# A prefix sum of row blocks: the last two groups by rows, with their columns taken by TensorE

## The chip, the cores and the metric

One core of a Trainium2 chip. The metric is the time of one execution on the device, in microseconds, as the median of several runs; lower is better. A profile gives the span from the first to the last instruction; measured times are about 1.7 us longer than it (677.9 against 676.2 for the run before).

## The reference

```python
def reference(x):                        # x: 4 x 4224 x 4224, float32
    ps = np.cumsum(np.cumsum(x, axis=1), axis=2)
    diag = np.diagonal(ps, axis1=1, axis2=2)
    return np.cumsum(diag, axis=1).astype(np.float32)
```

Only the diagonal of the 2-d prefix sum is wanted, and its running sum. A step of the diagonal from i-1 to i adds the new row up to the diagonal and the new column above it. So the kernel has to read every element once (285 MB) and form sums of rows left of the diagonal and sums of columns above it.

## The kernel before

The matrix of a batch is cut into 11 groups of 384 rows. A group is loaded as a strip, 128 partitions with 3 rows each. For each group

- ScalarE sums each row up to the end of the diagonal block (`act_sum`, which writes its input back in place);
- VectorE masks the diagonal block, sums what is above the diagonal, and adds the three rows into `u`, the running column sums;
- TensorE multiplies the group's 384 columns of `u` with a selecting weight, which puts their sum over the partitions into row k of `d` (`columns`).

The last batch ends otherwise: group 9 is loaded by rows, group 10 in pieces (`part_a`, `part_b`) whose sums on VectorE stand behind `d` in its queue: those of `part_a`'s first piece before the two scans of `d`, the rest after them. The names at the end: `r3` is what remains of the groups' row sums and goes into `d` too, `pu` and `c12` are sums and scans of `d`, `arows` and `bsum` the row sums of `part_a` and `part_b`, and `fin_a`, `fin_b`, `fin_e` the products that weigh them into the last results `yl` and `ye`.

```python
def act_sum(acc, src):
    nc.scalar.activation(out=src, in_=src, func=ACT.Copy, accum_out=acc)

def pair_sum(acc, src):            # VectorE adds two halves and accumulates
    w = src.shape[-1] // 2
    pair = dumpool.tile([P, 768], FP32, name="pair")
    nc.vector.scalar_tensor_tensor(out=pair[:, :w], in0=src[:, :w], scalar=1.0,
        in1=src[:, w:], op0=ALU.mult, op1=ALU.add, accum_out=acc)
# ... cut ...
for g in range(NG if whole else LG - 1):        # NG = 11, LG = 10
    # ... strip loaded whole ...
    for q in range(F):                          # F = 3
        act_sum(rsum[:, k, q : q + 1], strip[:, q, :hi])
    block = strip[:, :, lo:hi]
    nc.vector.tensor_mul(out=block, in0=block, in1=um3)
    row_sums(rabove[:, k, :], block)
    # ... group 0 cut: u = sum of the rows ...
    for q in range(F):
        add_to(u[:, lo:], strip[:, q, lo:])
    columns(g, u_of(g))
if not whole:
    columns(LG, head[:, 0, :])
    g = LG - 1
    # ... cut ...
    wa = 2304
    for q in range(F):
        load(out=strip[:, q, :], in_=rows_of(b, g)[:, q, :])
    for q in range(F):
        act_sum(rsum[:, k, q : q + 1], strip[:, q, :wa])
        pair_sum(more[:, q : q + 1], strip[:, q, wa:hi])
        block = strip[:, q, lo:hi]
        masked(block, block, um3[:, q, :], rabove[:, k, q : q + 1])
        add_to(u[:, lo:], strip[:, q, lo:])
    for j in (g, LG):
        columns(j, u_of(j))
    add_to(rsum[:, k, :], more)
# ... r3 into d, loads of group 10, pu and c12 from d, carry ...
        sum_a(1, *acuts[0], acuts[0][0] + 1536)   # ScalarE's share of part_a
# ... two scans, then ...
sum_a(3, *acuts[1], acuts[1][0] + 768)
# ... arows, fin_a, fin_b, then part_b and the end ...
```

## Time and profile before

| | before |
|---|---|
| time, median | 677.86 us (4 runs, 677.56 to 678.51) |
| span of the profiled run | 676.2 us |
| last piece of the input lands | 665.8 us |
| `d` ready, VectorE starts `pu` | 663.8 us |
| TensorE starts `fin_a` | 669.4 us |

The transfers set the pace up to 665.8; 10.4 us of the span lie after them. The lines that show it, and the chain of waits at the end, stand in the prediction below. One view that it tells in words is the table of stretches of 1 us. Its columns are the stretch, its length, the busy time with instruction counts of TensorE, its weight loads, VectorE, ScalarE and GpSimd, the granted TensorE clock, the transfer engines' share, and GB/s:

```profile
662.00:663.00 1.00, 1.00 (x4) 0.41 (x3) 0.00 (x0) 1.00 (x3) 0.00 (x0) 0.50 0.99 388
...
664.00:665.00 1.00, 0.04 (x2) 0.07 (x3) 1.00 (x4) 0.52 (x3) 0.00 (x0) 1.00 0.15 60
```

The second-last figure falls from 0.99 to 0.15: the stream is over. VectorE (the third pair) is idle at 662, waiting for `d`, just when it should work off what has landed.

### The profile page before, as it was taken

What the parts mean: (1) busy time and instruction counts of PE and PEld (TensorE: products, weight loads), DVE (VectorE), ACT (ScalarE), POOL (GpSimd) and SP (SyncE); (2) the same over time, 40 slices, a digit from 0 to 9 for tenths busy, and PEclk for the clock granted to TensorE, in tenths of its full rate; (3) what the DMA queues carried; (4) which work ended last, traced back from release to release, by engine and by line L of the source; (5) the groups of instructions that cost most, each with busy time, mean ns of one, the idle gap of its engine ahead of it and who ended that gap; (6) DMA issues with size and microseconds to landing.
All of it is one profiled execution on the core that took longest, in us unless ns stands there. A gap on an engine that the chain in (4) does not pass through costs nothing.

```text
span 676.2 us, 1095 instructions
## 1 busy us (share of the span) xinstructions
PE 73.6 (11%) x138; PEld 12.8 (2%) x138; DVE 449.0 (66%) x277; ACT 276.3 (41%) x275; POOL 35.0 (5%) x81
## 2 busy tenths in 40 slices
PE   0001100000010000000100000001101000001015
PEld 0000000000000000000000000000000000000002
DVE  3679766544379887655347988765334998875475
ACT  0023344456622233445761223346674122345673
POOL 5000000000000000000000000000000000001200
PEclk9999999999999999999999999999999555555556
DMA  9999999999999999999999999999999999999992
GB/s 371 432 435 435 432 435 435 435 441 435 438 435 432 435 432 432 432 432 432 432 432 432 432 432 432 432 435 432 432 432 432 435 432 432 432 432 430 416 418 101
DMA packets 7868, 285.62 MB, mean 422 GB/s; under 512 B 872, under 2 KB 1300, under 8 KB 1844
## 3 DMA queue, kind: packets, MB, share of 16 engines
q0 software_dynamic: 7392, 284.89, 97.7%
q1 hardware_dynamic: 468, 0.66, 0.3%
q14 instruction: 7, 0.06, 0.0%
q8 instruction: 1, 0.02, 0.0%
HBM read 285.47 MB, written 0.07 MB: 422 GB/s over the span
## 4 chain that ended last, share of the span: by engine, by line
DMA 73%; ACT 10%; DVE 9%; issue 6%; PE 2%; ACTq 0%; DVEq 0%; POOLq 0%
DMA strip<-in_x_dram 73%; ACT strip L211 10%; DVE u L231 4%; DVE u L300 1%; DVE strip L297 1%; DVE above L214 1%; PE d L205 1%; DVE pair L220 1%; DVE c L379 0%; PE fin_b L205 0%; DVE strip L234 0%; PE fin_a L205 0%; DVE pu L214 0%; DVE c L234 0%; ACTq L211 0%
## 5 line engine op out<-in xcount | busy, mean ns | idle before, releaser
L211 ACT ACTIVATE strip<-strip 128x768 f32<-128x768 f32 (+11 forms) x137 | 270.5, 1975 | 389.0 <-DMA strip<-in_x_dram 374.7
L231 DVE TENSOR_TENSOR u<-u,strip 128x3840 f32<-128x3840 f32 (+10 forms) x121 | 299.1, 2472 | 2.9
L297 DVE TENSOR_TENSOR strip<-strip,um 128x1152 f32<-128x1152 f32 x42 | 57.0, 1357 | 203.4 <-ACT strip L211 203.4
L205 PE MATMUL d<-u,sel 128*33 128x384 f32 (+1 forms) x88 | 65.0, 844 | 593.9 <-DVE u L231 593.9
L214 DVE TENSOR_REDUCE above<-strip 128x3 f32<-128x1152 f32 x42 | 56.8, 1353 | 1.5
L292 POOL DMA_DIRECT2D strip<-in_x_dram x39 | 20.7, 530 | 574.6 <-DVE u L231 535.8
L211 ACT ACTIVATION_READ_ACCUMULATOR strip<-strip 128x1 f32 x137 | 25.5, 186 | 0.0
L205 PEld LDWEIGHTS d<-u,sel 128*33 128x33 f32 (+1 forms) x88 | 7.6, 134 | 648.7 <-DVE u L231 647.7
L300 DVE TENSOR_TENSOR u<-strip 128x4224 f32<-128x4224 f32 x4 | 18.2, 4549 | 0.0
L220 DVE SCALAR_TENSOR_TENSOR pair<-strip 128x384 f32<-128x384 f32 (+5 forms) x12 | 6.9, 577 | 0.2
L214 DVE TENSOR_REDUCE pu<-d 33x1 f32<-33x384 f32 (+1 forms) x2 | 1.1, 548 | 6.1 <-PE d L205 6.1
L198 DVE TENSOR_SCALAR steps<-steps 128x128 int32<-128x128 int32 x1 | 0.2, 227 | 7.0 <-POOL steps L197 7.0
L352 POOL DMA_DIRECT2D strip<-in_x_dram x5 | 2.7, 552 | 4.7 <-DMA strip<-in_x_dram 4.7
L205 PE MATMUL d<-ones_all,r 128*33 128x128 f32 (+1 forms) x12 | 2.6, 377 | 0.0
L316 POOL DMA_DIRECT2D strip<-in_x_dram x3 | 1.6, 528 | 14.2 <-issue 14.2
L205 PE MATMUL fin_b<-weights,bsum 128*1 128x128 f32 (+2 forms) x12 | 2.1, 362 | 0.0
L341 POOL DMA_DIRECT2D strip<-in_x_dram x2 | 1.4, 709 | 13.2 <-issue 13.2
L379 DVE TENSOR_TENSOR_SCAN c<-ones_all,carry,c 33x384 f32<-33x384 f32 (+1 forms) x2 | 2.0, 1008 | 0.1
L379 DVE TENSOR_TENSOR_SCAN c<-ones_all,carry,d 33x384 f32<-33x384 f32 (+1 forms) x2 | 2.0, 1003 | 0.1
L205 PEld LDWEIGHTS d<-ones_all,r 128*33 128x33 f32 (+1 forms) x12 | 1.8, 154 | 2.2 <-issue 1.9
L205 PE MATMUL fin_a<-weights,arows 128*1 128x256 f32 (+1 forms) x4 | 1.4, 514 | 3.9 <-DVE arows L214 3.9
L86 POOL DMA_DIRECT2D strip<-in_x_dram x3 | 1.7, 594 | 0.8 <-POOLq L467 0.8
(67 smaller groups left out, 28.5 us busy)
## 6 DMA issues: line engine op xcount, KB each, us to landing
strip<-in_x_dram POOLq DMA_DIRECT2D x42, 6336.0 KB, 27.9
strip<-in_x_dram POOLq DMA_DIRECT2D x3, 2112.0 KB, 22.3
strip<-in_x_dram POOLq DMA_DIRECT2D x1, 2304.0 KB, 18.7
strip<-in_x_dram POOLq DMA_DIRECT2D x1, 1536.0 KB, 21.8
strip<-in_x_dram POOLq DMA_DIRECT2D x3, 480.0 KB, 23.0
head<-in_x_dram SPq DMA_DIRECT2D x1, 576.0 KB, 3.9
strip<-in_x_dram POOLq DMA_DIRECT2D x1, 352.0 KB, 23.7
strip<-in_x_dram POOLq DMA_DIRECT2D x1, 128.0 KB, 19.0
```

The costliest lines, as they stand in the source:

```text
L86: load(out=t, in_=rows_of(0, i))
L205: nc.tensor.matmul(o, lhsT=lhsT, rhs=rhs, start=start, stop=False, skip_group_check=True)
L211: nc.scalar.activation(out=src, in_=src, func=ACT.Copy, accum_out=acc)
L214: nc.vector.reduce_sum(out=acc, in_=src, axis=AX.X)
L220: nc.vector.scalar_tensor_tensor(out=pair[:, :w], in0=src[:, :w], scalar=1.0, in1=src[:, w:], op0=ALU.mult, op1=ALU.add, accum_out=acc,)
L231: nc.vector.tensor_add(out=o, in0=o, in1=i)
L292: load(out=strip, in_=rows_of(b, g))
L297: nc.vector.tensor_mul(out=block, in0=block, in1=um3)
L300: nc.vector.tensor_add(out=u, in0=strip[:, 0, :], in1=strip[:, 1, :])
L316: load(out=strip[:, q, :], in_=rows_of(b, g)[:, q, :])
L352: load(out=part_b[:, sb, c0:c1], in_=x[b, r0 : r0 + R, :NH].rearrange("r (k c) -> r k c", k=4)[:, :, c0:c1],)
L379: nc.vector.tensor_tensor_scan(out=c12[:, i, :], data0=ones_row[:rows], data1=src, initial=carry[:, i : i + 1], op0=ALU.mult, op1=ALU.add,)
```

## The change

The intent is to have VectorE ready when the last rows land. Groups 8 and 9 are loaded by rows; ScalarE sums only 2176 columns of each, so that VectorE's part doesn't wait for it; TensorE takes the columns from the strip itself, which saves the adds into `u`; and VectorE, now freer, gets more of the last sums. Group 0's row sums go from ScalarE to VectorE as well. The core of the diff (the `pair` tile grows from 768 to 896 columns, too):

```diff
-        for g in range(NG if whole else LG - 1):
+        for g in range(NG if whole else LG - 2):
 ...
+            if g == 0:
+                row_sums(rsum[:, k, :], block)
+            else:
+                for q in range(F):
+                    act_sum(rsum[:, k, q : q + 1], strip[:, q, :hi])
 ...
+            for j in range(LG - 2, NG):
+                columns(j, u_of(j))
             columns(LG, head[:, 0, :])
-            g = LG - 1
-            wa = 2304
 ...
-                add_to(u[:, lo:], strip[:, q, lo:])
-            for j in (g, LG):
-                columns(j, u_of(j))
+            wa = 2176
+            for i, g in enumerate((LG - 2, LG - 1)):
+                k, lo, hi = row_of(g), g * GW, (g + 1) * GW
+                strip = strip_tile()
+                for q in range(F):
+                    load(out=strip[:, q, :], in_=rows_of(b, g)[:, q, :])
+                for q in range(F):
+                    act_sum(rsum[:, k, q : q + 1], strip[:, q, :wa])
+                    pair_sum(more[:, i, q : q + 1], strip[:, q, wa:hi])
+                    block = strip[:, q, lo:hi]
+                    masked(block, block, um3[:, q, :], rabove[:, k, q : q + 1])
+                    for j in range(g + 1, NG):
+                        columns(j, strip[:, q, j * GW : (j + 1) * GW])
+                    columns(g, block)
+                add_to(rsum[:, k, :], more[:, i, :])
 ...
-            sum_a(1, *acuts[0], acuts[0][0] + 1536)
+            sum_a(1, *acuts[0], acuts[0][0] + 1216)
-        sum_a(3, *acuts[1], acuts[1][0] + 768)
+        sum_a(3, *acuts[1], acuts[1][0] + 640)
-        for k, ca in ((0, 480), (1, 480), (2, 416)):
+        for k, ca in ((0, 416), (1, 416), (2, 416)):
```

More of the change, by code (lines that the diff above doesn't have):

```diff
@@ L218, in pair_sum @@
         w = src.shape[-1] // 2
-        pair = dumpool.tile([P, 768], FP32, name="pair")
+        pair = dumpool.tile([P, 896], FP32, name="pair")
         nc.vector.scalar_tensor_tensor(
@@ L293 @@
             k, lo, hi = row_of(g), g * GW, (g + 1) * GW
-            for q in range(F):
-                act_sum(rsum[:, k, q : q + 1], strip[:, q, :hi])
             block = strip[:, :, lo:hi]
+            if g == 0:
[3 more added lines that the diff above has]
+                    act_sum(rsum[:, k, q : q + 1], strip[:, q, :hi])
             nc.vector.tensor_mul(out=block, in0=block, in1=um3)
@@ L307 @@
         if not whole:
+            for j in range(LG - 2, NG):
+                columns(j, u_of(j))
             columns(LG, head[:, 0, :])
-            g = LG - 1
-            k, lo, hi = row_of(g), g * GW, LG * GW
-            strip = strip_tile()
-            more = last.tile([P, F], FP32, name="more")
-            wa = 2304
-            for q in range(F):
-                load(out=strip[:, q, :], in_=rows_of(b, g)[:, q, :])
-            for q in range(F):
-                act_sum(rsum[:, k, q : q + 1], strip[:, q, :wa])
-                pair_sum(more[:, q : q + 1], strip[:, q, wa:hi])
-                block = strip[:, q, lo:hi]
-                masked(block, block, um3[:, q, :], rabove[:, k, q : q + 1])
-                add_to(u[:, lo:], strip[:, q, lo:])
-            for j in (g, LG):
-                columns(j, u_of(j))
-            add_to(rsum[:, k, :], more)
+            more = last.tile([P, 2, F], FP32, name="more")
+            wa = 2176
[13 more added lines that the diff above has]
+                add_to(rsum[:, k, :], more[:, i, :])
         if b < LB - 1:
```

## The prediction

> **What bounds the kernel now.** I read the page's slices first, to see whether any engine or the transfers are full:
>
> ```profile
> DVE  3679766544379887655347988765334998875475
> DMA  9999999999999999999999999999999999999992
> q0 software_dynamic: 7392, 284.89, 97.7%
> ```
>
> The transfer engines are at nine tenths or more in 39 of 40 slices, and queue 0 takes 97.7% of the span. No compute engine is full over the run (VectorE 66%, ScalarE 41%, TensorE 11%). So up to the last bytes the kernel can't become faster by any saving of instructions: the change moves the same bytes. What can be saved is the time between the last landing and the end. Next I looked for when the last bytes come: in stretches of one microsecond the transfer share falls from 0.99 (662 to 663 us) to 0.34 and 0.15; the issues by line show the last piece (128 KB) issued at 646.81 and landing 19.0 us later, at 665.8. The span is 676.2. So 10.4 us at the end run without transfers. The chain of waits, in order of time, says what fills the end:
>
> ```profile
> 608.94 27.49 DMA strip<-in_x_dram
> 636.54 5.00 ACT strip L211 x3
> 642.59 3.26 ACT strip L211 x3
> 645.88 1.37 DVE strip L297
> 647.27 1.35 DVE above L214
> ...
> 660.14 3.64 PE d L205 x10
> 663.80 0.55 DVE pu L214
> ...
> 669.44 1.44 PE fin_a L205 x4
> 670.88 2.76 PE fin_b L205 x16
> 673.66 0.29 DVE yl L418
> ...
> 674.04 0.18 DVE ye L451
> ```
>
> From 636.5 the chain isn't DMA any more. Group 8 lands whole at 636.5; ScalarE sums its three rows of 3456 columns in place until 645.9; only then may VectorE mask the block, and it is 8 us late from there on. The timeline of that stretch shows it:
>
> ```profile
> 645.88 1.36 DVE L297 TENSOR_TENSOR strip<-strip,um 128x1152 f32<-128x1152 f32 x1 [7.97 <-ACT strip L211]
> 648.54 4.13 DVE L231 TENSOR_TENSOR u<-u,strip 128x1152 f32<-128x1152 f32 x3
> 651.63 2.12 ACT L211 ACTIVATE strip<-strip 128x2304 f32<-128x2304 f32 x1 [1.57 <-DMA strip<-in_x_dram]
> 652.59 0.95 DVE L220 SCALAR_TENSOR_TENSOR pair<-strip 128x768 f32<-128x768 f32 x1
> 660.14 2.73 PE L205 MATMUL d<-u,sel 128*11 128x384 f32 x4 [4.68 <-DVE u L231]
> ```
>
> VectorE starts group 9 at 652.6 though its last row landed at 651.6, ends it at 660.1, TensorE makes d until 663.8, and everything that VectorE still owes (sums of part_a and part_b) stands behind d in its queue.
>
> **What the Trainium skill says.** "DMA: Bandwidth & Descriptors", Where 436 GB/s comes from, puts the ceiling of this path at 435.2 GB/s; the page's slices show 432 to 435 nearly throughout, so it agrees and the stream has no reserve. "VectorE: DVE Perf Modes", The perf-mode tier table, has fp32 tensor_tensor at 1x, one element a cycle: here 384 columns take 0.56 us and 768 take 0.95, a slope of 1.0 ns a column, which agrees; I size the new pair sums by it. "TensorE: Matmul & The Clock Gate", What's actually happening: the array runs at 1.2 GHz until it has been busy about 3.4 us, then at 2.4, and falls back after such a window of idleness. The trace agrees at the end: TensorE is busy from 660.14, the granted clock goes from 0.50 to 1.00 at about 663.2, and back to 0.50 at about 666.6; at 1.00 a 128x128 half took 270 ns, at 0.50 it took 418. (The 0.97 of the first 558 us I don't believe: the 384-column halves took 848 ns there and 831 later at 0.50.) "FP8 and Floating Point Precision" tells of four passes for a true fp32 product; no separate run shows passes here, but one column call is two MATMULs, issued 0.63 us apart at clock 0.50, 1.27 us a call.
>
> **The change, part by part.**
>
> Loading: group 8 in three row pieces of 2112 KB. Group 9's already went so, at 641.6, 646.7 and 651.6, 5.0 us apart, 15.1 for the strip where whole strips take 15.0. Group 8's rows should land at about 626.5, 631.5, 636.5. Cost 0 to 0.1 us. The GpSimd queue waits on earlier landings for its last issues; by the order of waits of both kernels, the last two pieces wait for the first and second row of group 9 in both, so the last landing stays 665.8.
>
> Group 0's sums: 3 activations (3 x 0.5 us) become one reduction of 1152 columns, 1.35 us, on VectorE in each batch. In the last batch VectorE is behind there: its group 2 ends at 564.4 and then idles 1.75 us for ScalarE. 1.35 fits into 1.75, and the strips in flight reach to 546 while the delayed load would be issued at 537. Worth 0.
>
> ScalarE in groups 8 and 9: it is done with group 7 at 629.9. Six sums of 2176 columns at about 2.0 us plus the readout, against 3 x 3.07 and 3 x 2.12 before: rows 8 end at 632, 634.1, 638.7, rows 9 at 643.7, 648.7, 653.8 (landing plus 2.2).
>
> VectorE: removed are, for group 8, the mask (1.37), the reduction (1.35) and three adds (4.13), for group 9 three adds of 0.96; added are three pair sums of width 640 (0.86 start to start), three masks (0.60), and pair sums of 832 in place of 768 (1.06 against 0.99). Group 8 costs 3 x 1.46 = 4.4 in place of 6.85, and, as the pair sums and masks read columns that ScalarE does not touch, it starts when VectorE is free of group 7, at 637.9, not at 645.9: done 642.4. Group 9 then goes with its landings, 644.1, 648.2, 653.3. The row sums are whole at 653.9, r3 at 654.1; before, 660.2.
>
> TensorE: from 637.95 it has 5 calls (u 7 to 10 and head), then 9 for group 8, 6 for group 9, where it had 5 in all from 652.7. 20 calls at 1.27 would be 25.4 us, 663.4. But it is busy without a gap from 637.95, so I expect the clock to rise at about 641.5; the 2.7 calls done by then leave 11.3 of the first 14, at 0.65 us (half of 1.27, an estimate) 7.3 us: 648.8. Group 9's six then follow their rows, the last block at about 653.9; r3 0.6 to 1.1. d is ready at about 655.0 against 663.8: 8.8 us earlier.
>
> The end: pu and c12 1.2, 656.2. The next in VectorE's queue, the pair sums of part_a, wait for a landing at 657.25; two of width 544 at 0.75: 658.75. Carry and two scans 2.2: 661.0. Second piece (660.95), two of width 448 at 0.65: 662.3; arows 662.55. TensorE starts fin_a at 662.75 instead of 669.44. From fin_a's start to the finish of fin_b took 673.66 - 669.44 = 4.22 us, TensorE without a gap; part_b's pieces land at 662.6 to 665.5 and the pair sums of width 272 take 0.46, so the inputs come in time: 666.97. VectorE is done with the last piece (665.8 + 0.4 + what stands before it) at 666.3, just earlier. From there to the end before: 676.2 - 673.66 = 2.54. New span 669.5, a gain of 6.7; measured times are 1.7 above the span (677.87 against 676.2): 671.2. Of the 8.8 us won at d, 1.0 goes to the wait for part_a at 657.25, the rest to wider sums and landings. The cuts of ScalarE's share cost VectorE 2 x 0.17 + 2 x 0.07 + 2 x 0.03, about 0.5 us, and it has waits to put them in.
>
> **The rivals.** First, TensorE stays cold in the run of 20 calls: d at 663.4 plus 1.1, 664.6, 0.8 later than before, and the wider pair sums add 0.5 behind it: 679. For: it has never been busy longer than 4 us in this trace, and at 652.73 to 655.46, busy 2.7 us, it stayed at 0.50. Against: both bursts over 3 us ended at 1.00. A part of it (clock rises late, or falls between group 9's rows) costs 1 to 3 us, of which the wait for part_a hides the first: 671.5 to 674. Second, the landings hide the gain: the end can't be before 665.8 + 0.4 (last pair sum) + 0.3 (fin_e) + 2.3 (ye to the end), 668.8, time 670.5. That's only 0.7 below my figure, so it is a floor and not another outcome. Third, the smaller loads or the later strip release slow the stream: 0.1 to 0.5 us per group seen against; the page's slice with group 9's rows has 416 GB/s against 432, which would be 0.6: 671.8.
>
> **Range and chances.** The floor is near below, the rivals stretch upward: 671.2, eight in ten within 670.3 to 673.6. Faster by 2% would be 664.3, below the floor: 0.01. Slower by 2% is 691.4; even the cold case is far from it: 0.01.
>
> **What would show it.** Right: the last landing still near 665.8; VectorE's first group 8 pair sum at about 638 with no wait for ScalarE; granted clock at 1.00 from about 641 to 655; pu near 655 followed by a wait for a transfer; fin_a near 662.8. Wrong: column halves still 0.63 us apart after 645, pu after 660, or transfers below 430 GB/s between 605 and 660.

## The result, and the profile after

The changed kernel took 671.43 us (4 runs, 670.94 to 671.47) against 677.86; the ratio is 0.9902, with a 95% interval from 0.9885 to 0.9919. A ratio here and below is the mean time of one kernel's fast runs over that of the kernel before in the same rounds, so it is not quite the ratio of the medians quoted. Predicted were 671.2, within 670.3 to 673.6. The span is 669.7 (predicted 669.5).

The chain of waits of the changed kernel, in order of time (start, length, what):

```profile
626.90 6.94 ACT strip L211 x7
...
639.12 21.96 DMA strip<-in_x_dram
...
662.74 0.17 DVE arows L214
...
662.96 1.44 PE fin_a L205 x4
664.40 2.76 PE fin_b L205 x16
...
667.18 0.29 DVE yl L424
...
667.56 0.18 DVE ye L457
```

The long run of VectorE and TensorE pieces from 645.9 to `fin_a` at 669.4 is gone. Between 639 and 661 the chain is a transfer again: that of `part_a`'s second piece. After it come ScalarE's sums, `arows`, and the same 4.2 us of products (`fin_a`, `fin_b`) as before, 6.5 us sooner: 662.96 against 669.44.

The timeline of the changed kernel, whose brackets give how long the engine idled before and for whom:

```profile
637.78 0.82 DVE L220 SCALAR_TENSOR_TENSOR pair<-strip 128x640 f32<-128x640 f32 x1
637.92 5.30 PE L205 MATMUL d<-u,sel 128*11 128x384 f32 x8 [13.32 <-DVE u L231]
643.70 9.19 PE L205 MATMUL d<-strip,sel 128*11 128x384 f32 x28
...
651.73 1.02 DVE L220 SCALAR_TENSOR_TENSOR pair<-strip 128x832 f32<-128x832 f32 x1 [3.43 <-DMA strip<-in_x_dram]
653.41 0.82 PE L205 MATMUL d<-strip,sel 128*11 128x384 f32 x2 [0.52 <-DVE strip L234]
655.18 0.55 DVE L214 TENSOR_REDUCE pu<-d 11x1 f32<-11x384 f32 x1 [0.92 <-PE d L205]
657.32 0.72 DVE L220 SCALAR_TENSOR_TENSOR pair<-strip 128x544 f32<-128x544 f32 x1 [1.12 <-DMA strip<-in_x_dram]
661.11 0.63 DVE L220 SCALAR_TENSOR_TENSOR pair<-strip 128x448 f32<-128x448 f32 x1 [0.15 <-DMA strip<-in_x_dram]
662.74 0.16 DVE L214 TENSOR_REDUCE arows<-asum 128x2 f32<-128x10 f32 x1 [0.33 <-ACT strip L211]
666.36 0.29 DVE L220 SCALAR_TENSOR_TENSOR pair<-strip 128x128 f32<-128x128 f32 x1 [0.25 <-DMA strip<-in_x_dram]
667.18 0.28 DVE L424 TENSOR_TENSOR yl<-fin_b,c 1x128 f32<-1x128 f32 x1 [0.52 <-PE fin_b L205]
```

VectorE starts group 8 at 637.78 with no wait for ScalarE, and in group 9 it now waits for the rows (3.43 us for the last one). `pu` starts at 655.18 instead of 663.80, 8.6 us sooner; behind it VectorE waits 1.12, 0.15 and 0.33 us, which together with 0.5 us of wider sums is what the 8.6 us lose on the way to 6.5. TensorE's row of 28 halves (a call is two MATMULs, its halves) has no gap: 14 calls in 9.19 us. That is the full clock, as the stretches say:

```profile
643.00:644.00 1.00, 1.00 (x4) 0.32 (x3) 0.52 (x2) 0.80 (x2) 0.00 (x0) 0.96 0.95 406
...
660.00:661.00 1.00, 0.00 (x0) 0.00 (x0) 0.96 (x1) 0.00 (x0) 0.00 (x0) 0.58 1.06 426
```

The granted clock, the third figure from the end, is 0.50 until 643.1, then 1.00 (0.96 is the mean of that microsecond), and falls back at 660.2 (0.58 of that one).

### The profile page after: what moved, and what is told of

It is laid out like the page before. It is cut to its first block, busy times and chain, and to the rows that moved or that the text cites. A ratio compares the mean times of both kernels' runs of the same rounds, so it can differ in the third digit from the quotient of the medians.

```text
span 669.7 us, 1134 instructions
## 1 busy us (share of the span) xinstructions
PE 82.4 (12%) x168; PEld 15.6 (2%) x168; DVE 449.8 (67%) x286; ACT 265.6 (40%) x251; POOL 36.1 (5%) x83
## 4 chain that ended last, share of the span: by engine, by line
DMA 66%; ACT 16%; DVE 13%; issue 2%; PE 1%; POOL 0%; ACTq 0%; DVEq 0%; POOLq 0%
DMA strip<-in_x_dram 66%; ACT strip L211 16%; DVE u L231 5%; DVE u L303 3%; DVE strip L300 2%; DVE above L214 2%; DVE sums L214 1%; PE d L205 0%; PE fin_b L205 0%; DVE c L385 0%; PE fin_a L205 0%; POOL strip L347 0%; ACTq L211 0%; DVE pu L214 0%; DVE c L234 0%
## 5 line engine op out<-in xcount | busy, mean ns | idle before, releaser
L211 ACT ACTIVATE strip<-strip 128x768 f32<-128x768 f32 (+14 forms) x125 | 260.1, 2081 | 399.8 <-DMA strip<-in_x_dram 374.2
L231 DVE TENSOR_TENSOR u<-u,strip 128x3840 f32<-128x3840 f32 (+10 forms) x115 | 292.2, 2541 | 2.7
L211 ACT ACTIVATION_READ_ACCUMULATOR strip<-strip 128x1 f32 x125 | 23.3, 186 | 0.0
L220 DVE SCALAR_TENSOR_TENSOR pair<-strip 128x640 f32<-128x640 f32 (+6 forms) x15 | 10.2, 679 | 9.0 <-DMA strip<-in_x_dram 8.9
L205 PE MATMUL d<-strip,sel 128*11 128x384 f32 x30 | 10.0, 486 | 0.5 <-DVE strip L234 0.5
L214 DVE TENSOR_REDUCE sums<-strip 128x3 f32<-128x1152 f32 x4 | 5.4, 1341 | 6.0 <-DMA strip<-in_x_dram 6.0
L234 DVE SCALAR_TENSOR_TENSOR strip<-strip,um 128x384 f32<-128x384 f32 x6 | 3.3, 558 | 0.2
L205 PEld LDWEIGHTS d<-strip,sel 128*11 128x11 f32 x30 | 2.7, 93 | 7.7 <-issue 6.0
```

Source lines behind the costliest of these rows:

```text
L205: nc.tensor.matmul(o, lhsT=lhsT, rhs=rhs, start=start, stop=False, skip_group_check=True)
L214: nc.vector.reduce_sum(out=acc, in_=src, axis=AX.X)
L231: nc.vector.tensor_add(out=o, in0=o, in1=i)
L234: nc.vector.scalar_tensor_tensor(out=o, in0=i, scalar=1.0, in1=m, op0=ALU.mult, op1=ALU.mult, accum_out=acc,)
```

## The experiments

Theory A, from the prediction: the gain comes from VectorE being on time; two things put it there (it no longer waits for ScalarE in group 8, and it adds nothing into `u`), and TensorE can take the columns only because its clock rises. Rivals: one of the two is the real cause; the clock is not needed; the new shares at the end do it. Each run below was timed in five rounds against the kernel before. Every result was correct.

**e1: rows and shares kept, adds and columns as before.**

```diff
-            for j in range(LG - 2, NG):
-                columns(j, u_of(j))
-                    for j in range(g + 1, NG):
-                        columns(j, strip[:, q, j * GW : (j + 1) * GW])
-                    columns(g, block)
+                    add_to(u[:, lo:], strip[:, q, lo:])
+                columns(g, u_of(g))          # and columns(LG, u_of(LG)) after group 9
```

> Groups 8 and 9 by rows and the new cuts as in the change, but VectorE adds the rows to u and TensorE takes u's columns, as before. Theory A (the gain comes from VectorE no longer waiting for ScalarE's in-place sums of group 8; the columns from the strip are the smaller half): VectorE needs 2.8 us a row in group 8 (637.8 to 646.2) and 2.6 a row in group 9, last add at 654.35, two cold calls of 1.27 and r3: pu at 658.1 instead of 655.2, fin_a at 664.7 instead of 663.0, time 673.2. Theory B (TensorE's columns from the strip are what gains): nearly all of the 6.5 us is lost, 676 to 678.

Measured: 672.95 us (672.35 to 673.43), ratio 0.9924. The timeline:

```profile
651.87 1.02 DVE L220 SCALAR_TENSOR_TENSOR pair<-strip 128x832 f32<-128x832 f32 x1 [0.51 <-DMA strip<-in_x_dram]
...
658.44 0.55 DVE L214 TENSOR_REDUCE pu<-d 11x1 f32<-11x384 f32 x1 [3.64 <-PE d L205]
...
664.56 1.44 PE L205 MATMUL fin_a<-weights,arows 128*1 128x256 f32 x4 [4.40 <-DVE arows L214]
```

VectorE, adds and all, has caught up by the last row: it waits 0.51 us for it. Freeing it from ScalarE alone brings `pu` to 658.4. What then remains is TensorE's two cold calls and `r3` behind the last add. Theory A's figures (658.1, 664.7, 673.2) hold; theory B falls.

**e2: columns from the strip, but group 8 loaded whole and summed by ScalarE in place.**

```diff
+                if i == 0:                   # group 8
+                    load(out=strip, in_=rows_of(b, g))
+                    for q in range(F):
+                        act_sum(rsum[:, k, q : q + 1], strip[:, q, :hi])
+                    # ... cut: tensor_mul of the block and row_sums, as before the
+                    # change; columns j > g of the three rows, then of the block ...
+                    continue
                 for q in range(F):           # group 9, as in the change
                     load(out=strip[:, q, :], in_=rows_of(b, g)[:, q, :])
```

> TensorE takes the columns of groups 8 and 9 from the strip, but group 8 is loaded whole, ScalarE sums all its 3456 columns in place and VectorE waits for that, as before. Both changes alone remove enough from VectorE's queue: it starts at 645.9, masks and reduces until 648.6, has group 9's rows at 650.3, 652.0 and 653.6, so pu stays within 0.3 of 655.2 and the time within 0.4 of 671.4. If Theory A's stronger form holds (the wait for ScalarE must go), the time is 674 to 677.

Measured: 671.19 us (670.83 to 671.35), ratio 0.9899, no slower than the change's 0.9902.

```profile
645.76 1.36 DVE L326 TENSOR_TENSOR strip<-strip,um 128x1152 f32<-128x1152 f32 x1 [7.96 <-ACT strip L211]
651.51 1.03 DVE L220 SCALAR_TENSOR_TENSOR pair<-strip 128x832 f32<-128x832 f32 x1
654.97 0.55 DVE L214 TENSOR_REDUCE pu<-d 11x1 f32<-11x384 f32 x1 [0.92 <-PE d L205]
```

VectorE waits 7.96 us for ScalarE, as in the kernel before, and it costs nothing: without the adds (4.1 us in group 8, 2.9 in group 9) it reaches the last row just as that lands (651.5), and `pu` is where the change has it. So each half of the change alone (with the rest of it kept) brings VectorE to the last row in time. Taking the columns off it is enough for the whole gain; loading group 8 by rows is enough for some 5.3 us (678.25 to 672.95). The stronger form of theory A, that the wait must go, falls.

**e3: every call on a strip doubled, with weights of zero.**

```diff
+        def nothing(rhs):
+            matmul(d, sel[:, :rows], rhs)    # these columns of sel are zero
 ...
                     for j in range(g + 1, NG):
                         columns(j, strip[:, q, j * GW : (j + 1) * GW])
+                        nothing(strip[:, q, j * GW : (j + 1) * GW])
                     columns(g, block)
+                    nothing(block)
```

> The change, with each of the 15 calls on the strips followed by a call of the same shape with weights of zero (the result stays right). At the full clock a doubled call costs what one would at half the clock: 30 calls x 0.64 = 19.2 us from 643.4 give 662.6, pu at about 663.4 instead of 655.2. Theory (the rise of TensorE's clock carries the gain): time 677.5 to 678.3, as slow as the kernel before. Rival (TensorE has slack enough, the clock is not needed): within 0.5 of 671.4.

Measured: 678.11 us (677.03 to 679.16), ratio 1.0001 (0.9988 to 1.0013): the whole gain is gone. The chain:

```profile
637.93 25.06 PE d L205 x76
...
663.02 0.55 DVE pu L214
```

TensorE is the chain for 25 us. A doubled call at the full clock lasts as long as a single one at half of it (0.32 us against 0.64 a half), so this is about what the change would be if the clock stayed low: no gain. It shows that the change rests on the rise of the clock as far as a doubling can stand for a low clock; the clock itself can't be held down without changing what TensorE does.

**e4: the old shares of ScalarE at the end.**

```diff
-            sum_a(1, *acuts[0], acuts[0][0] + 1216)
+            sum_a(1, *acuts[0], acuts[0][0] + 1536)
-        sum_a(3, *acuts[1], acuts[1][0] + 640)
+        sum_a(3, *acuts[1], acuts[1][0] + 768)
-        for k, ca in ((0, 416), (1, 416), (2, 416)):
+        for k, ca in ((0, 480), (1, 480), (2, 416)):
```

> The change with the old shares of ScalarE in the last sums (1536, 768, 480, 480, 416). arows then waits for ScalarE's second sum of 768 columns, 0.2 us later than that of 640: 671.6, plus 0.1 to 0.3. If the cuts matter more than that, above 672; if they don't matter, 671.4.

Measured: 671.42 us (671.04 to 671.75), ratio 0.9902. In its trace `arows` starts 1.85 us after the second piece's sums begin (661.21 to 663.06), in the change 1.63 (661.11 to 662.74). So the mechanism is there with the size expected, 0.2 us, but the time doesn't tell it from the change. The shares are worth nothing that could be measured.

**e5: group 0's row sums on ScalarE again.** (The `if g == 0` branch of the diff undone.)

> The change, with group 0's row sums on ScalarE again, as before. They lie in a stretch where the transfers set the pace: theory 0 (671.4, within 0.3). If the time rises by more than 0.5, ScalarE's or VectorE's queue at the start of a batch reaches the end after all.

Measured: 671.54 us (671.2 to 672.47), ratio 0.9897. No effect that the times show. The changed kernel's timeline shows why, and how near it was:

```profile
566.04 1.36 DVE L300 TENSOR_TENSOR strip<-strip,um 128x1152 f32<-128x1152 f32 x1 [0.36 <-ACT strip L211]
```

At this place the kernel before idled 1.75 us; the 1.35 us more of VectorE's work in group 0 have eaten all but 0.36 of it.

**e6: nine idle calls ahead of the last products.**

```diff
         weigh_b(dtot[:, 2:3], weights, M0, start=True)
+        idle_ps = psum_s.tile([11, GW], FP32, name="idle_ps")
+        for i in range(9):
+            matmul(idle_ps, sel[:, :11], u[:, :GW], start=i == 0)
```

> The change, with nine calls of 384 columns on weights of zero into a bank of their own between dtot's product and fin_a (656.9 to about 662.7), so that TensorE's clock stays high for the last products. Theory (the last 4.2 us of products at half the clock and the last landing at 666.3 end nearly together): fin_b is done before the last pair sum, and the end moves by only 0.3 to 0.5: time 671.0. Rival 1 (the products alone set the end): the chain of 4.2 us shrinks to 2.5, time 669.7. Rival 2 (landing alone): 671.4.

Measured: 670.92 us (670.8 to 673.0; three of the four at most 671.01), ratio 0.9897. In its chain the products are no longer what ends last:

```profile
646.75 19.35 DMA strip<-in_x_dram
...
666.19 0.31 DVE pair L220 x2
...
666.54 0.23 PE fin_e L205 x2
...
666.80 0.18 DVE ye L460
```

The first product on `bsum` starts 1.1 us after `fin_a` (662.78 to 663.86) where it took 2.1 in the change (662.96 to 665.05), and the last landing holds the end. The last products at half the clock and the last landing end within half a microsecond of each other, as expected.

**e7: the kernel before with only the new shares at the end.** (The last hunk of the diff and the wider `pair` tile, nothing else.)

> The kernel before with only the new end cuts (1216, 640, 416). VectorE is behind d there, so the wider pair sums stand on the path: 2 x 0.17 before the carry, 2 x 0.07 before arows: 0.4 to 0.5 us slower than before, ratio 1.0006. If ScalarE's share was what held the end of the kernel before, it is faster.

Measured: 678.7 us (678.51 to 680.11), ratio 1.0009 (0.9996 to 1.0021). From `pu` to `fin_a` it takes 6.11 us (664.33 to 670.44), in the kernel before 5.64 (663.80 to 669.44): 0.47 more, as expected. The time alone doesn't show a difference. The shares are no gain by themselves. With e7 the four cases stand together: neither half 678.7 us, rows alone 672.95 (e1), columns alone 671.19 (e2), both 671.43 (medians, not all of the same rounds). e7 also keeps the old 2304 columns of group 9 on ScalarE, a difference that no run tests alone.

**e8: six idle calls in TensorE's queue behind group 8.**

```diff
+                if i == 0:
+                    for q in range(2 * F):
+                        nothing(u_of(q))
                 add_to(rsum[:, k, :], more[:, i, :])
```

> The change with six calls on weights of zero after group 8's columns, 3.9 us at the full clock. If TensorE has the slack that the trace shows (0 to 0.7 us of waits for group 9's rows, and 1.1 us of VectorE's wait for part_a behind d), 2.1 to 2.8 of it reach the end: 673.5 to 674.2. With more slack: 671.4 to 672.5.

Measured: 672.09 us (671.72 to 672.71), ratio 0.9908; the expected 673.5 to 674.2 was a miss, and the time lies in the range that was named for more slack. The six calls are in TensorE's timeline from 648.5 to 652.4; behind them VectorE's:

```profile
657.13 0.55 DVE L214 TENSOR_REDUCE pu<-d 11x1 f32<-11x384 f32 x1 [3.02 <-PE d L205]
...
663.02 0.16 DVE L214 TENSOR_REDUCE arows<-asum 128x2 f32<-128x10 f32 x1
```

`pu` comes 1.95 us later than in the change, so TensorE's own slack took 1.95 of the 3.9, where 0 to 0.7 had been counted. Part of that is the run's: here the clock rose at 641.3, in the profile from which the slack was read at 643.1, and the calls on the strips start at 642.73 instead of 643.70. `arows` comes only 0.28 later: behind `pu` the queue has 1.67 us of slack, the three waits together (1.12 + 0.15 + 0.33 = 1.60), where I had counted only the first. Two other runs agree: in e1 `pu` is 3.26 later than in the change and `fin_a` 1.60, in e3 7.84 and 6.17; the difference is 1.66 and 1.67.

**e9, e10, e11: the change again, the idle calls of e6 again, and the idle calls on top of e2, on one chip in the same rounds.** (No new edits.)

> The change itself, unaltered, on the same chip as the two next runs, so that half a microsecond can be told: 671.4, span 669.7.

> The kernel with nine idle calls ahead of the last products a second time, beside the change: 0.4 to 0.6 below it if the products at half the clock and not only the last landing hold the end; equal if the landing alone does.

> Group 8 loaded whole with its columns taken by TensorE, and the nine idle calls. Since loading whole cost nothing, as the kernel with the idle calls: 0.4 to 0.6 below the change. If one of the two needs the other, above the change.

Measured: e9 671.28 (671.22 to 671.44), e10 670.98 (670.82 to 671.16), e11 670.56 (670.34 to 671.04); ratios 0.9901, 0.9896, 0.9892. The idle calls gain 0.3 us, somewhat under the 0.4 to 0.6 expected. e9's profile shows how close the race is: the clock happened to rise at 666.0 instead of 667.0, the products on `bsum` took 1.46 us instead of 2.09, and the chain of the unaltered change ends in the last landing there, not in the products. Group 8 loaded whole is a further 0.4 lower in the median, which I had not expected; the runs of e10 and e11 overlap (670.82 to 671.16, 670.34 to 671.04), so the times alone don't settle it. In e11 VectorE takes the last piece at 665.97 without a wait for its landing, in e10 it waits for it until 666.37:

```profile
666.37 0.29 DVE L220 SCALAR_TENSOR_TENSOR pair<-strip 128x128 f32<-128x128 f32 x1 [0.25 <-DMA strip<-in_x_dram]
```

```profile
665.97 0.29 DVE L220 SCALAR_TENSOR_TENSOR pair<-strip 128x128 f32<-128x128 f32 x1
```

(The first line is e10's timeline, the second e11's.) The landings show what lies behind it. Counted from the landing of group 7, the last piece lands after 44.4 to 44.5 us in the four profiles with group 8 loaded whole (the kernel before, e2, e7, e11), and after 44.6 to 44.9 in the nine with three loads. Of these 0.1 to 0.5 us, 0.15 are there when group 8 is complete (15.15 us after group 7 instead of 15.00); the last piece's issue, which waits for a row of group 9, then comes 8.5 us after `part_a`'s first instead of 8.3. Where the rest comes from is open. e11 is the fastest version, 0.7 us or 0.1% below the change and with no overlap of their runs; no run here tries for more.

## Why the prediction was right

- **The bound and the floor.** It said that only the 10.4 us behind the last landing can be saved. The landing moved by only 0.5 us (665.8 expected, 666.3 found) and the end came to within about 3.4 us of it. One sign of being wrong did come up, transfers below 430 GB/s between 605 and 660: they moved 421 GB/s there, but 423 in the kernel before as well, so the mark was set too high to tell anything.
- **VectorE's part.** Group 8 from 637.9 without ScalarE (found 637.78), the last mask done by 653.3 (found 653.4, when TensorE starts on it), r3 at 654.1 (found 654.06).
- **TensorE's part.** The clock was to rise at 641.5; in the profiled run it rose at 643.1. That made the first 14 calls end at about 649.5 (the head's calls end the cold stretch at 643.7, nine calls at 0.65 follow) instead of 648.8, and it cost nothing: the four calls on group 9's first two rows follow without a gap and end at about 652, just as the last row is there (651.7). That the moment of the rise could be missed by 1.6 us without harm was partly luck: it came 2.8 us (e4) to 5.2 us (this profile) after the start of the calls, where 3.5 had been counted, and with 5.2 no slack was left before the last row. e10, which keeps the change up to `d`, had the rise 2.0 us earlier, at 641.1, and has `pu` at 655.19, the change at 655.18. `pu` was expected at 655.0 and came at 655.18. The first rival, a clock that stays low, had about the right size, with e3's doubled calls as a stand-in: 679 expected for it, 678.1 measured. (A slip on which nothing rests: by its timeline, the kernel before had four calls from 652.7, not five; the fifth stood at 637.96.)
- **The end.** The wait for `part_a` until 657.25 (found 657.32), `arows` at 662.55 (found 662.74, 0.33 of it for ScalarE), `fin_a` at 662.75 (found 662.96), `fin_b`'s finish at 666.97 (found 667.18). Each is 0.1 to 0.2 late, and the sum of them is the 0.2 us by which the span was missed.
- **What was mis-sized.** "Cost 0 to 0.1 us" for the row loads, with the last landing unmoved: the landings of nine profiles against four put it at 0.15 us when group 8 is complete and 0.1 to 0.5 at the last landing (told at e11). That `arows` would wait 0.33 us for ScalarE was not in the sum either. e8's expectation, made later, counted the slack behind `d` as one wait, where there are three, and TensorE's own slack too small.
- **What the prediction didn't see.** It treated "no wait for ScalarE" and "no adds" as one sum. They overlap: e2 has the whole gain without the first, e1 most of it without the second, because VectorE can't be earlier than the last row's landing at 651.7. In the change VectorE waits 3.43 us for that row; that is the part paid for twice.

## What to carry to other kernels

When a kernel is bound by a stream, ask what each engine still owes when the last bytes land, and aim to have every queue empty just then; once an engine waits for the last landing, further relief of it is worth nothing, and one of two remedies was enough. Work handed to an idle TensorE must be sized at the clock that it will have there: 20 calls at half the clock, 25 us by the prediction's estimate, would have eaten the gain; 19 of them took 15 (637.9 to 652.9) because a run of calls without a gap raised it, and the last one waited for its row. Before counting an added delay as lost, add up all the waits behind it in the same queue.

## What the Trainium skill lacked or had wrong

- "TensorE: Matmul & The Clock Gate", Back-to-back issue gap, gives N/1.2 and N/2.4 + 2.5 ns for one matmul alone and no figure for fp32. Here one fp32 call of 384 columns is two MATMULs, issued 0.64 us apart at half the clock and 0.32 at the full one, 1.28 and 0.65 a call. That is four times the page's gap (an estimate from its formula: 4 x 320 and 4 x 162.5 ns), which agrees with the four passes that "FP8 and Floating Point Precision", TensorE Precision Notes, tells of; no run here shows the passes themselves.
- The same page, What's actually happening, puts the rise at about 3.4 us of activity, give or take 0.5 us. In the ten profiles here in which the calls on the strips follow, TensorE's queue always started with the same five calls, and the clock rose 2.8 us (e4, 638.02 to 640.84) to 5.2 us (the change, 637.92 to 643.08) after their start; the issues come closer just then. So the scatter is wider (the section also says that the number of slow calls differs between runs). That the window runs freely agrees: within a profile the recorded changes lie whole multiples of 3.41 us apart (643.08, 660.15 and 666.98 in the change). A window with 2.7 us of TensorE's work in it raised the clock (e1, 638.05 to 640.79, rise at 641.04), one with 2.5 us did not (the kernel before, 652.98 to 656.39).
- The same page, Seeing it yourself, warns that the records of the clock can be unreliable, without saying how. Here the granted clock before a profile's first recorded change can't be used: in e1 that change is at 641.04, and from 636 on it reads 1.00, while a call of two halves at 638.05 took 1.45 us, just as it does at 0.50. The spacing of issues decides.
- None of the pages cited here says what splitting a load costs when others are queued behind it: row loads of 2112 KB land 5.05 us apart, nearly the pace of a whole strip (15.0), yet three of them in place of group 8's single load went with group 8 complete 0.15 us later and the last landing 0.1 to 0.5 us later (nine profiles against four).
